# Reordering the opening of a decoder layer: modulation weights, first projection weights, constants and the order of the first products

## The chip, the cores and the metric

The kernel runs on one core of a Trainium2 chip. The metric is device time in microseconds of one execution; before the change the median of three runs is 1246.67 us (1246.11 to 1247.33). All times below are in microseconds unless marked otherwise.

## The reference, cut to what matters

The layer takes x (512 tokens by 1024 channels) and a conditioning vector c. What the change touches is its first step: a layer norm, scaled and shifted by a function of c, then one large projection.

```python
c_act = jax.nn.silu(c)
mod = c_act @ ada_w[l] + ada_b[l]
sh1, sc1, g1, sh2, sc2, g2 = jnp.split(mod, 6, axis=-1)
h = _layer_norm(x) * (1 + sc1[:, None]) + sh1[:, None]
proj = h @ w_in[l] + b_in[l]
```

Behind it stand gated recurrence, sparse attention, a merge, and a mixture of experts; none of their code is changed.

## The kernel before

[...] Tiles come from rings: 36 buffers of 128x1024 floats ("Q"), 24 of 128x512 ("S"), and the 8 banks of PSUM.

**Loads.** The SyncE queue issues, in this order: the four 128-token tiles of x (`xt`), the modulation weights of part 0 (`ada_fetch(0)`, four tiles `adaw` of 512 KB), the first half of the first projection block (`first[0].fetch1()`, 512 KB, four of the eight k-tiles of 128 channels), modulation part 1, the first halves of the second and third block, modulation part 2, the three second halves, modulation part 3, and the block `kw_block`. ScalarE's queue loads c, biases and the table `cst` (identity, triangle, counter: 256.5 KB). GpSimd's queue loads bias rows, then the constants `cmpc` of the later compression step; at the end of the opening stage it also loads `rel_bias` and the bucket table (lines 550 and 554).

**From x to its transpose.** For each x tile VectorE takes statistics (line 229, two halves, then line 231), ScalarE makes the reciprocal deviation (lines 233, 234), VectorE a small product (line 404), ScalarE applies it to the tile (line 405, `x_norm`, line 402). Then `c_silu` runs three small ScalarE steps and three small VectorE steps. Then `x_transposed` (line 407 on) transposes each tile on TensorE; VectorE and ScalarE copy two halves of each bank into `xT` (lines 413, 414). Last come the columns of biases (`colT`, `ncolT`, lines 427, 430).

**Modulation.** `modulation(c)` multiplies silu(c) with the 16 weight pieces of part c. The four pairs of shift or scale (s) and channel half (j) write to four places of 32 columns of the TensorE array, so that products of different places can run side by side. The loop has k outermost, so four neighbouring calls go to four places. VectorE copies the result to `mrow` (line 459); `modulate(c)` brings it into columns by two small products (line 181, `pg<-sel,mrow`) and an addition (line 466, `modc`); ScalarE makes the high part `hh` of two k-tiles of h (line 469), VectorE the full value `hk` (line 471) and the low part `hl` (line 472).

**First products.** Weights are split into high and low parts too (`split1`: ScalarE line 280 gives `wh`, VectorE line 282 gives `wl`). For the first half of `first[0]` the subtraction of line 282 runs on GpSimd. Six PSUM banks `fps` (two for each of three blocks) collect 144 products: for each part c of two k-tiles, for each bank f, the three products wh·hh, wh·hl, wl·hh of both k-tiles, the one with `hl` second. The next modulation is issued ahead of bank 2, its `modulate` ahead of bank 3, so 18 products stand between `modulate(c+1)` and the first product that reads its result.

After that stage follow the products of `kw_block` and, woven in by estimated durations, the compression step and the bias rows (`bias_rows`, line 547 on).

Of the kernel before, what the change touches and what calls it, by code (L numbers as in the profile page):

```python
# [21 lines left out]
F32 = mybir.dt.float32  # L22
F32R = mybir.dt.float32r
# [3 lines left out]
AF = mybir.ActivationFunctionType  # L27
OP = mybir.AluOpType
# [15 lines left out]
C_ID, C_TRI, C_IOTA, C_VAL, C_N = 0, 128, 256, 512, 513  # L44
# [24 lines left out]
MOD_F = 2  # L69
# [71 lines left out]
def hybrid_kernel(ctx, tc, a, out, dbg=None, stop=None):  # L141
    nc = tc.nc
# [7 lines left out]
    cp = ctx.enter_context(tc.tile_pool(name="cp", bufs=1))  # L150
# [5 lines left out]
    def Q(name, dt=F32):  # L156
        return big.tile([128, 1024], dt, name=name, tag="Q", bufs=36)
# [33 lines left out]
    xt = [Q("xt") for i in range(NT)]  # L191
# [4 lines left out]
    A.dma_start(rowa[16:24, :], a["c"][0].rearrange("(r p) -> r p", p=128))  # L196
    A.dma_start(rowa[0:16, :], a["ada_b"][0, 0:2048].rearrange("(r p) -> r p", p=128))
    cst = cp.tile([128, C_N], F32, name="cst")
    A.dma_start(cst, a["cst"])
    A.preload_act_table_set("natural_log_exp_and_others")  # L200

    rows = S("rows")[:, 0:128]
# [5 lines left out]
    P_.dma_start(rows[93:94, :], a["cmp_b1_v"][0][None, :])  # L208

    cmpc = S("cmpc")  # L210
    P_.dma_start(cmpc[:, 0:128], a["cmp_w2_k"][0])
    P_.dma_start(cmpc[:, 128:256], a["cmp_w2_v"][0])
    P_.dma_start(cmpc[0:32, 256:384], a["cmp_pos_k"][0])
    P_.dma_start(cmpc[0:32, 384:512], a["cmp_pos_v"][0])
    ident = cst[:, C_ID:C_ID + 128]
    tri = cst[:, C_TRI:C_TRI + 128]
    iota = cst[:, C_IOTA:C_IOTA + 256]
# [7 lines left out]
    def layer_stats(src, pre, st=None, later=False):  # L225
        if st is None:
            st = small(pre + "st", 12)
            for q in range(2):
                V.bn_stats(st[:, q * 6:(q + 1) * 6], src[:, q * 512:(q + 1) * 512])
        mv = small(pre + "mv", 2, bufs=4 if pre == "l0" else 2)  # L230
        V.bn_aggr(mv, st.rearrange("p (q s) -> p q s", s=6))
        rs = small(pre + "rs", 2, bufs=4 if pre == "l0" else 2)
        A.activation(rs[:, 0:1], mv[:, 1:2], AF.Ln, bias=eps[:, 0:1])
        A.activation(rs[:, 0:1], rs[:, 0:1], AF.Exp, scale=-0.5)
        if not later:
            V.scalar_tensor_tensor(rs[:, 1:2], mv[:, 0:1], -1.0, rs[:, 0:1], op0=OP.mult, op1=OP.mult)
        return mv, rs
# [125 lines left out]
    def ada_fetch(c):  # L363
        t = []
        for s in range(2):
            u = []
            for j in range(2):
                w = Q("adaw").rearrange("p (k n) -> p k n", k=4)
                nc.sync.dma_start(w, ada[:, 4 * j:4 * j + 4, s * 1024 + c * 256:s * 1024 + (c + 1) * 256])
                u.append(w)  # L370
            t.append(u)
        adw.append(t)

    ada_fetch(0)
    first[0].fetch1()
    ada_fetch(1)
    first[1].fetch1()
    first[2].fetch1()
    ada_fetch(2)
    for b in first:  # L380
        b.fetch1()
    ada_fetch(3)
    kw_block = Block(wview, KW)
    kw_block.fetch()

    prow = PS("prow")
    tr(prow[:, 0:24], rowa[:24, :], ident[:24, :24])
# [11 lines left out]
    xT = [Q("xT").rearrange("p (k t) -> p k t", k=2) for _ in range(4)]  # L399
    stats = {}  # L400

    def x_norm(i):
        mv, rs = stats[i]
        V.scalar_tensor_tensor(rs[:, 1:2], mv[:, 0:1], -1.0, rs[:, 0:1], op0=OP.mult, op1=OP.mult)
        A.activation(xt[i], xt[i], AF.Identity, bias=rs[:, 1:2], scale=rs[:, 0:1])

    def x_transposed(i):
        for k4 in range(2):
            pt = PS("pxT")
            for k in range(4):  # L410
                tr(pt[:, k * 128:(k + 1) * 128], xt[i][:, (4 * k4 + k) * 128:(4 * k4 + k + 1) * 128], ident)
            src = pt.rearrange("p (k t) -> p k t", k=4)
            V.tensor_copy(xT[2 * k4][:, :, i * 128:(i + 1) * 128], src[:, 0:2])
            A.activation(xT[2 * k4 + 1][:, :, i * 128:(i + 1) * 128], src[:, 2:4], AF.Copy)
    for i in range(NT):
        stats[i] = layer_stats(xt[i], "l0", later=True)
        if i:
            x_norm(i - 1)
    x_norm(NT - 1)
    c_silu()  # L420
    for i in range(NT):
        x_transposed(i)

    prow2 = PS("prow2")
    tr(prow2[:, :94], rows[:94, :], ident[:94, :94])
    colT = cp.tile([128, 94], F32, name="colT")
    V.tensor_copy(colT, prow2[:, :94])
    b1k, b1v = colT[:, 92:93], colT[:, 93:94]
    ncolT = cp.tile([128, 68], F32, name="ncolT")
    V.tensor_scalar(ncolT, colT[:, :68], -1.0, None, op0=OP.mult)  # L430

    def bcol(off):
        j = off // 128 if off < 6656 else 52 + (off - MGH) // 128
# [3 lines left out]
        j = off // 128 if off < 6656 else 52 + (off - MGH) // 128  # L437
        return ncolT[:, j:j + 1]

    hh = halves("hh")  # L440
    hl = halves("hl")
    modc = cp.tile([128, 2, 8], F32, name="modc")
    fps = [PS("pfirst") for _ in range(6)]
    pg = PS("pg")
    pc = pg[:, 256:272].rearrange("p (k s) -> p s k", s=2)
    mrow = S("mrow")[:, 0:256]

    sel = small("sel", 2, bufs=1)
    V.tensor_add(sel, ident[:, 0:65:64], ident[:, 32:97:64])

    def modulation(c):

        for k in range(4):
            for s in range(2):
                for j in range(2):
                    r = 64 * s + 32 * j
                    mm(pg[r:r + 32, 0:256], cT[:, 4 * j + k:4 * j + k + 1].to_broadcast([128, 32]), adw[c][s][j][:, k, :],
                       k == 0, k == 3, pos=(0, r))
        V.tensor_copy(mrow, pg[:, 0:256])

    def modulate(c):

        for q in range(2):
            mm(pg[:, 256 + 4 * c + 2 * q:258 + 4 * c + 2 * q], mrow[:, q * 128:(q + 1) * 128], sel, True, True)
        cs = slice(2 * c, 2 * c + 2)
        V.tensor_add(modc[:, :, cs], pc[:, :, cs], modb[:, :, cs])
        for k in (2 * c, 2 * c + 1):
            xk = xT[k // 2][:, k % 2, :]
            A.activation(hh(k), xk, AF.Identity, bias=modc[:, 0, k:k + 1], scale=modc[:, 1, k:k + 1])
            hk = S("hk")  # L470
            V.tensor_scalar(hk, xk, modc[:, 1, k:k + 1], modc[:, 0, k:k + 1], op0=OP.mult, op1=OP.add)
            V.tensor_sub(hl(k), hk, hh(k).bitcast(F32))
            if k == 3:
                probe("hk3", hk)

    modulation(0)
    first[0].split1(P_)
    modulate(0)
    for c in range(4):
        if c % 2 == 0:  # L480
            for b in first:
                if len(b.h) <= c // 2:
                    b.split1()
        for f in range(6):
            b = first[f // 2]
            if f % 2 and c == 3 and f < 5:
                kw_block.split1()
            if f == MOD_F and c < 3:
                modulation(c + 1)
            if f == MOD_F + 1 and c < 3:  # L490
                modulate(c + 1)
            for k in (2 * c, 2 * c + 1):
                three_k(fps[f], lambda k: b.H(k, (f % 2) * 128, 128), lambda k: b.L(k, (f % 2) * 128, 128), hh, hl, k)
    probe("modc", modc)


# [50 lines left out]
    def bias_rows():  # L547
        rbT = small("rbT", 8, bufs=1)
        rb = small("rb", 32, bufs=1)
        P_.dma_start(rb[0:8, :], a["rel_bias"])  # L550
        bk = [S("buck") for _ in range(3)]
        for j in range(3):
            wd = 512 if j < 2 else 256
            P_.dma_start(bk[j][0:32, :wd], a["buck"][:, j * 512:j * 512 + wd])
        yield 3000

        def bkc(c, n, rows):
            j, o = divmod(c, 512)
# [12 lines left out]

        P_.dma_start(ext2_d, ext_d[:, None, :].to_broadcast([8, 128, 640]))
# [1265 lines left out]
```

## Time and profile before

| what | value |
|---|---|
| median of three runs | 1246.67 us |
| the profiled execution, own time | 1247.05 us |
| its span, first to last instruction | 1245.3 us |
| mean granted TensorE clock | 0.986 |
| PE busy | 1169.0 us, 94% of the span |
| DVE busy | 685.0 us, 55% |
| ACT busy | 438.4 us, 35% |
| POOL busy | 82.8 us, 7% |

The profile gives one execution. The rows below are read as follows: a line of the timeline is one instruction or a merged run of like ones; the bracket at its end tells how long its engine had stood idle and what released it.

### The profile page before, as it was taken

The numbers are of one execution on the slowest core, as the hardware profiler recorded it, in microseconds if no ns is written. First come the engines' busy times: TensorE is split into PE (matmuls) and PEld (weight loads), VectorE is DVE, ScalarE is ACT, GpSimd is POOL, SyncE is SP. The second block draws the span as 40 slices with busy tenths as digits, with TensorE's granted clock in tenths as the row PEclk, the third lists the DMA queues.
The fourth block names the chain that finished last, engine by engine and source line by source line (L and its number), as shares of the span: only waits on it lengthen the run. The fifth ranks groups of instructions, "written<-read, shape, count | busy, mean of one in ns | idle before, by whom it ended". The sixth has DMA issues, their size and how long they took to land. (4 is left out here: it accounts for less than half of the span.)

```text
span 1245.3 us, 18172 instructions
## 1 busy us (share of the span) xinstructions
PE 1169.0 (94%) x6455; PEld 802.1 (64%) x6455; DVE 685.0 (55%) x1626; ACT 438.4 (35%) x916; POOL 82.8 (7%) x164
## 2 busy tenths in 40 slices
PE   5999999989999999999999979999999899999985
PEld 3788798778888888878877773435435235355322
DVE  5564888787665656322586678435125144444314
ACT  4333656764444353555222541201102001112013
POOL 3011111111011011002000110000000000000000
PEclk9999999999999999999999989999999999999997
DMA  9955324134244234236155199999999999999991
GB/s 325 307 142 156 89 78 127 49 131 133 83 149 122 76 121 136 85 102 194 60 192 169 57 349 348 410 408 410 409 409 408 409 409 409 408 407 401 409 355 71
DMA packets 137629, 296.10 MB, mean 238 GB/s; under 512 B 11195, under 2 KB 74883, under 8 KB 137536
## 3 DMA queue, kind: packets, MB, share of 16 engines
q1 hardware_dynamic: 128224, 268.57, 58.9%
q0 software_dynamic: 8544, 23.97, 6.1%
q10 hardware_dynamic: 768, 2.37, 0.6%
q8 instruction: 52, 0.85, 0.3%
q14 instruction: 41, 0.34, 0.1%
HBM read 292.73 MB, written 4.76 MB: 239 GB/s over the span
## 5 line engine op out<-in xcount | busy, mean ns | idle before, releaser
L183 PE MATMUL p<-ew,xe 128*32 128x512 f32 (+1 forms) x960 | 194.7, 597 | 11.6 <-DMA ew<-in_exp_w_dram 11.6
L282 DVE TENSOR_TENSOR wl<-wst,wh 128x1024 fp32r<-128x1024 f32 (+1 forms) x93 | 109.3, 1201 | 74.2 <-ACT wh L280 73.4
L183 PEld LDWEIGHTS p<-ew,xe 128*32 128x32 f32 (+1 forms) x960 | 53.2, 122 | 146.4 <-issue 83.5
L183 PE MATMUL py<-ew,aT 128*32 128x512 f32 (+1 forms) x464 | 98.6, 598 | 8.7 <-DMA ew<-in_exp_w_dram 5.4
L1545 DVE TENSOR_TENSOR s<-s,p 128x512 f32<-128x512 f32 x13 | 8.9, 688 | 176.4 <-PE p L183 160.7
L280 ACT ACTIVATE wh<-wst 128x1024 fp32r<-128x1024 f32 (+1 forms) x94 | 93.2, 1030 | 29.7 <-DVE wst L271 17.5
L183 PEld LDWEIGHTS py<-ew,aT 128*32 128x32 f32 (+1 forms) x464 | 24.8, 121 | 74.7 <-issue 37.0
L1553 ACT ACTIVATE aT<-pat 128x512 f32<-128x512 f32 x13 | 7.8, 597 | 177.3 <-PE pat L187 177.3
L1594 DVE TENSOR_TENSOR acc<-acc,pcb 128x512 f32<-128x512 f32 x96 | 58.3, 681 | 7.9 <-PE pcb L181 7.9
L1568 ACT ACTIVATE yh<-y 128x512 fp32r<-128x512 f32 x26 | 16.4, 630 | 126.7 <-DVE y L1566 126.7
L181 PE MATMUL pgx<-pm,xhh 128*128 128x256 f32 (+1 forms) x224 | 57.5, 301 | 0.0
L181 PE MATMUL pgx<-pm,xhl 128*128 128x256 f32 (+1 forms) x224 | 55.4, 292 | 0.0
L1566 DVE SCALAR_TENSOR_TENSOR y<-py,cs,g2b 128x512 f32<-128x512 f32 x26 | 19.4, 748 | 57.3 <-PE py L183 57.0
L181 PE MATMUL pmg<-hh,wh 128*128 128x512 f32 x128 | 50.4, 394 | 0.0
L181 PE MATMUL psg<-hh,wh 128*128 128x512 f32 x128 | 50.3, 393 | 0.0
L181 PE MATMUL psg<-hl,wh 128*128 128x512 f32 x128 | 49.9, 390 | 0.0
L181 PE MATMUL psg<-hh,wl 128*128 128x512 f32 x128 | 49.9, 390 | 0.0
L181 PE MATMUL pmg<-hh,wl 128*128 128x512 f32 x128 | 49.8, 389 | 0.0
L181 PE MATMUL pmg<-hl,wh 128*128 128x512 f32 x128 | 49.8, 389 | 0.0
L181 PEld LDWEIGHTS pgx<-pm,xhh 128*128 128x128 f32 x224 | 45.3, 206 | 6.5 <-issue 5.6
L181 PE MATMUL pcb<-yh,pT 128*128 128x512 f32 x104 | 43.7, 420 | 5.3 <-ACT sq L1722 5.3
L521 POOL DMA_DIRECT2D adaw<-in_ada_w_dram x64 | 34.6, 542 | 197.3 <-PE ptp L187 43.4
(552 smaller groups left out, 2777.6 us busy)
## 6 DMA issues: line engine op xcount, KB each, us to landing
ew<-in_exp_w_dram SPq DMA_DIRECT2D x380, 512.0 KB, 10.1
wst<-in_w_in_dram SPq DMA_DIRECT2D x66, 512.0 KB, 4.7
adaw<-in_ada_w_dram POOLq DMA_DIRECT2D x64, 256.0 KB, 3.1
adaw<-in_ada_w_dram SPq DMA_DIRECT2D x16, 512.0 KB, 9.2
wst<-in_w_br_hg_dram SPq DMA_DIRECT2D x8, 512.0 KB, 4.9
wst<-in_w_br_nsa_dram SPq DMA_DIRECT2D x8, 512.0 KB, 3.5
wst<-in_w_out_dram SPq DMA_DIRECT2D x8, 512.0 KB, 5.5
ext_d<-ext_d POOLq DMA_DIRECT2D x1, 2560.0 KB, 17.3
```

What stands on the lines that cost most here:

```text
L181: PE.matmul(o, l, r, start=start, stop=stop)
L183: PE.matmul(o, l, r, start=start, stop=stop, tile_position=pos)
L280: A.activation(wh, self.w[j], AF.Copy)
L282: (sub or V).tensor_sub(wl, self.w[j], wh.bitcast(F32))
L521: P_.dma_start(w, ada[:, k, 2048 + j * 512:2560 + j * 512])
L1545: V.tensor_mul(s1, s1, p3)
L1553: A.activation(aT, at_.rearrange("p (f s) -> p f s", f=4), AF.Copy)
L1566: V.scalar_tensor_tensor(y, py, cs_, g2b[c0 // 512][:, c0 % 512:c0 % 512 + n], op0=OP.mult, op1=OP.mult)
L1568: A.activation(yh, y, AF.Copy)
L1594: V.tensor_add(acc[i][:, s_], acc[i][:, s_], pc_)
```

## The change

- The first half of `first[0]` is loaded in two parts of two k-tiles (256 KB each). The first part goes ahead of modulation part 0, the second behind the first halves of the other two blocks; these three go ahead of modulation part 1. The parts are split one by one (`f0_split`), by ScalarE and VectorE; GpSimd does no subtraction any more.
- ScalarE's queue loads only the identity of `cst` (64 KB). The rest of it and `cmpc` are loaded by SyncE's queue behind `kw_block`. `rel_bias` and the bucket table are loaded by SyncE's queue too.
- The order from x to its transpose: the small product and the shift of tile i-1 stand between the two statistics halves of tile i; `c_silu` stands between tile 2 and tile 3; transposes and copies of tile 0 precede the shift of tile 3; `f0_split(0)` stands ahead of the copies of tile 3.
- `modulation` has k innermost, so that the four products of one place follow one another. In part 0 its copy to `mrow` and the addition into `modc` are made in two pieces.
- The products go by pairs of banks: for each k-tile wh·hh for both banks, then wl·hh, then wh·hl. The next modulation is issued ahead of banks 2 and 3 (in part 0 ahead of banks 4 and 5), its `modulate` behind the first k-tile of that pair.

```diff
-    A.dma_start(cst, a["cst"])
+    A.dma_start(cst[:, :C_TRI], a["cst"][:, :C_TRI])
...
+    def late_constants():
+        nc.sync.dma_start(cst[:, C_TRI:], a["cst"][:, C_TRI:])
+        nc.sync.dma_start(cmpc[:, 0:128], a["cmp_w2_k"][0])
...
+    def f0_fetch(k):
+        nc.sync.dma_start(f0w[:, k:k + 2], wview[:, k:k + 2, KC:KC + 256])
+
+    def f0_split(k):
+        A.activation(f0h[:, k:k + 2], f0w[:, k:k + 2], AF.Copy)
+        V.tensor_sub(f0l[:, k:k + 2], f0w[:, k:k + 2], f0h[:, k:k + 2].bitcast(F32))
+
+    f0_fetch(0)
     ada_fetch(0)
-    first[0].fetch1()
-    ada_fetch(1)
+    first[0].w.append(f0w)
     first[1].fetch1()
     first[2].fetch1()
+    f0_fetch(2)
+    ada_fetch(1)
     ada_fetch(2)
...
     kw_block.fetch()
+    late_constants()
...
+    def x_stats(i):
+        st = small("l0st", 12)
+        for q in range(2):
+            V.bn_stats(st[:, q * 6:(q + 1) * 6], xt[i][:, q * 512:(q + 1) * 512])
+            if q == 0 and i:
+                x_shift(i - 1)
+        stats[i] = layer_stats(xt[i], "l0", st=st, later=True)
...
-    for i in range(NT):
-        stats[i] = layer_stats(xt[i], "l0", later=True)
-        if i:
-            x_norm(i - 1)
-    x_norm(NT - 1)
+    x_stats(0)
+    x_stats(1)
+
+    V.tensor_add(sel, ident[:, 0:65:64], ident[:, 32:97:64])
+    x_stats(2)
     c_silu()
-    for i in range(NT):
-        x_transposed(i)
-
+    x_stats(3)
+    x_transposed(0)
+    x_shift(3)
+    x_transposed(1)
     prow2 = PS("prow2")
     tr(prow2[:, :94], rows[:94, :], ident[:94, :94])
+    pg = PS("pg")
+    x_transposed(2)
...
+    f0_split(0)
...
+    x_transposed(3)
     V.tensor_copy(colT, prow2[:, :94])
+    V.tensor_scalar(ncolT, colT[:, :68], -1.0, None, op0=OP.mult)
...
     def modulation(c):
 
-        for k in range(4):
-            for s in range(2):
-                for j in range(2):
-                    r = 64 * s + 32 * j
+        for s in range(2):
+            for j in range(2):
+                r = 64 * s + 32 * j
+                for k in range(4):
                     mm(pg[r:r + 32, 0:256], cT[:, 4 * j + k:4 * j + k + 1].to_broadcast([128, 32]), adw[c][s][j][:, k, :],
                        k == 0, k == 3, pos=(0, r))
-        V.tensor_copy(mrow, pg[:, 0:256])
+        for q in range(1 if c else 2):
+            w = slice(0, 256) if c else slice(q * 128, (q + 1) * 128)
+            V.tensor_copy(mrow[:, w], pg[:, w])
...
+    def first_products(fs, k, js=range(3)):
+
+        for j in js:
+            for f in fs:
+                b, w = first[f // 2], (f % 2) * 128
+                l, r = ((b.H, hh), (b.L, hh), (b.H, hl))[j]
+                mm(fps[f], l(k, w, 128), r(k), start=k == 0 and j == 0, stop=k == KT - 1 and j == 2)
+
     modulation(0)
-    first[0].split1(P_)
     modulate(0)
     for c in range(4):
-        if c % 2 == 0:
+        if c == 0:
+            first[1].split1()
+            first[2].split1()
+        if c == 2:
             for b in first:
-                if len(b.h) <= c // 2:
-                    b.split1()
...
+        for f in range(0, 6, 2):
+            if f == (2 if c else 4) and c < 3:
+                modulation(c + 1)
+            if f == 2 and c == 0:
+                f0_split(2)
...
             for k in (2 * c, 2 * c + 1):
-                three_k(fps[f], lambda k: b.H(k, (f % 2) * 128, 128), lambda k: b.L(k, (f % 2) * 128, 128), hh, hl, k)
+                first_products((f, f + 1), k)
+                if f == (2 if c else 4) and k == 2 * c and c < 3:
+                    modulate(c + 1)
...
-        P_.dma_start(rb[0:8, :], a["rel_bias"])
+        nc.sync.dma_start(rb[0:8, :], a["rel_bias"])
...
-            P_.dma_start(bk[j][0:32, :wd], a["buck"][:, j * 512:j * 512 + wd])
+            nc.sync.dma_start(bk[j][0:32, :wd], a["buck"][:, j * 512:j * 512 + wd])
```

## Rows read from the trace of the kernel before

**Rows 1.** The page: its first line, and from its second part the busy tenths of TensorE in 40 equal slices of the span.

```profile
span 1245.3 us, 18172 instructions
...
PE   5999999989999999999999979999999899999985
```

**Rows 2.** Busy time by stretches of the span. Columns: stretch in us, its length, busy us and instructions in brackets of PE, PEld, DVE, ACT and POOL, granted TensorE clock as a share of full speed, DMA share, GB/s.

```profile
0.00:16.40 16.40, 6.51 (x34) 4.94 (x34) 7.73 (x26) 9.03 (x19) 5.45 (x14) 1.00 0.92 312
16.40:27.10 10.70, 7.28 (x48) 4.66 (x48) 7.43 (x15) 5.80 (x11) 4.48 (x5) 0.84 1.11 344
27.10:61.80 34.70, 34.70 (x229) 26.49 (x229) 19.47 (x37) 10.28 (x13) 0.00 (x0) 1.00 1.05 313
```

**Rows 3.** Who waited for whom between 0 and 55 us: waiting engine, tile and line, what it waited for; us in total, times, longest.

```profile
DVE cT L394 <- ACT ce L243: 2.6, 1, 2.6
...
PE pfirst L181 <- DVE hl L472: 1.8, 1, 1.8
```

**Rows 4.** The timeline from the end of the first modulation to the second one. Columns: start us, duration us, engine, line, operation, output and input, shape, count, idle time before it with its releaser.

```profile
18.42 0.42 DVE L459 COPY mrow<-pg 128x256 f32<-128x256 f32 x1
...
19.39 2.35 POOL L282 TENSOR_TENSOR wl<-wst,wh 128x1024 fp32r<-128x1024 f32 x1 [11.11 <-ACT wh L280]
19.55 0.16 DVE L466 TENSOR_TENSOR modc<-pg,modb 128x4 f32<-128x4 f32 x1 [0.70 <-PE pg L181]
19.75 1.52 ACT L469 ACTIVATE hh<-xT,modc 128x512 fp32r<-128x512 f32 x2 [0.45 <-DVE modc L466]
19.75 2.27 DVE L471 TENSOR_SCALAR hk<-xT,modc 128x512 f32<-128x512 f32 x1
...
20.61 0.50 PE L181 MATMUL pfirst<-hh,wh 128*128 128x512 f32 x1 [1.10 <-ACT hh L469]
...
22.73 0.54 DVE L471 TENSOR_SCALAR hk<-xT,modc 128x512 f32<-128x512 f32 x1
...
22.87 0.80 PE L181 MATMUL pfirst<-hl,wh 128*128 128x512 f32 x1 [1.75 <-DVE hl L472]
...
27.14 1.93 PE L183 MATMUL pg<-adaw,cT 128*32 128x256 f32 x32
...
29.00 0.50 PE L181 MATMUL pfirst<-hh,wh 128*128 128x512 f32 x1
```

**Rows 5.** Busy time by stretches, columns as in Rows 2, around the time when the granted clock changed.

```profile
22.50:23.00 0.50, 0.13 (x1) 0.14 (x1) 0.50 (x2) 0.00 (x0) 0.50 (x2) 0.81 1.10 346
23.00:26.00 3.00, 3.00 (x7) 2.21 (x8) 0.96 (x2) 0.76 (x1) 0.86 (x2) 0.50 1.10 348
26.00:26.50 0.50, 0.50 (x3) 0.44 (x2) 0.17 (x1) 0.30 (x1) 0.00 (x0) 0.78 1.14 365
```

**Rows 6.** The timeline of the way from x to the transposed x (statistics, shift, sigmoid, copies), columns as in Rows 4.

```profile
6.03 0.29 ACT L233 ACTIVATE l0rs<-l0mv,eps 128x1 f32<-128x1 f32 x1 [2.58 <-DVE l0mv L231]
6.35 0.20 ACT L234 ACTIVATE l0rs<-l0rs 128x1 f32<-128x1 f32 x1
...
8.20 1.29 DVE L229 BATCH_NORM_STATS2 l0st<-xt 128x6 f32<-128x512 f32 x2 [0.74 <-DMA xt<-in_x_dram]
...
12.04 2.36 ACT L405 ACTIVATE xt<-xt,l0rs 128x1024 f32<-128x1024 f32 x2
...
14.31 0.15 ACT L241 ACTIVATE ce<-prow 128x8 f32<-128x8 f32 x1
...
14.98 0.16 DVE L394 TENSOR_TENSOR cT<-ce,prow 128x8 f32<-128x8 f32 x1 [2.65 <-ACT ce L243]
...
15.65 2.70 ACT L414 ACTIVATE xT<-pxT 128x256 f32<-128x256 f32 x8 [0.71 <-DVE xT L413]
...
17.86 0.25 DVE L427 COPY colT<-prow 128x94 f32<-128x94 f32 x1
```

**Rows 7.** The products of the first modulation: its row of the timeline; stretches of 0.05 us with the records of line 183 in flight in brackets, PE first and weight loads (PEld) second; then, from the timeline of a later stage, ten records of 128 columns that share one place in the array.

```profile
16.42 1.93 PE L183 MATMUL pg<-adaw,cT 128*32 128x256 f32 x32
...
16.60:16.65 0.05, 0.05 (x4) 0.00 (x0) 1.00 1.17 369
16.65:16.70 0.05, 0.05 (x8) 0.04 (x4) 1.00 1.14 348
16.80:16.85 0.05, 0.05 (x8) 0.00 (x0) 1.00 1.13 348
...
16.90:16.95 0.05, 0.05 (x8) 0.05 (x4) 1.00 1.16 369
...
72.00 1.25 PE L181 MATMUL pext<-buck,rbT 32*8 32x128 f32 x10
```

**Rows 8.** Transfers: the last tile of the first modulation's weights (issue, then time to landing, the answer for that tile between 6.5 and 8.5 us), two splits that waited for their weights, the SyncE queue's issues for the compression weights, and the first transpose that needs the bias table.

```profile
L369 SPq DMA_DIRECT2D adaw<-in_ada_w_dram x1: 2293/2293/2293, 5.6 to 5.6; - x1
...
DMA to landing us min/median/max: 10.6/10.6/10.6
...
25.24 1.06 ACT L280 ACTIVATE wh<-wst 128x1024 fp32r<-128x1024 f32 x1 [3.98 <-DMA wst<-in_w_in_dram]
...
26.78 1.06 ACT L280 ACTIVATE wh<-wst 128x1024 fp32r<-128x1024 f32 x1 [0.48 <-DMA wst<-in_w_in_dram]
...
45.97 6.96 SPq L261 DMA_DIRECT2D wst<-in_cmp_w_k_dram  x4
...
70.22 0.18 PE L187 MATMUL prb<-cst,rb 8*32 8x8 f32 x1
```

More of the change, by code (lines that the diff above doesn't have):

```diff
@@ L210, in hybrid_kernel @@
     cmpc = S("cmpc")
[L211 to L214, printed above, removed]
+    def late_constants():
+        nc.sync.dma_start(cst[:, C_TRI:], a["cst"][:, C_TRI:])
+        nc.sync.dma_start(cmpc[:, 0:128], a["cmp_w2_k"][0])
+        nc.sync.dma_start(cmpc[:, 128:256], a["cmp_w2_v"][0])
+        nc.sync.dma_start(cmpc[0:32, 256:384], a["cmp_pos_k"][0])
+        nc.sync.dma_start(cmpc[0:32, 384:512], a["cmp_pos_v"][0])
     ident = cst[:, C_ID:C_ID + 128]
@@ L372, in ada_fetch @@
         adw.append(t)
+    f0w = Q("wst").rearrange("p (k n) -> p k n", k=4)
+    f0h = f0l = None
+    def f0_fetch(k):
[4 more added lines that the diff above has]
+    f0_fetch(0)
     ada_fetch(0)
-    first[0].fetch1()
-    ada_fetch(1)
+    first[0].w.append(f0w)
     first[1].fetch1()
     first[2].fetch1()
+    f0_fetch(2)
+    ada_fetch(1)
     ada_fetch(2)
@@ L400, in hybrid_kernel, with x_shift @@
     stats = {}
-    def x_norm(i):
+    def x_stats(i):
[5 more added lines that the diff above has]
+        stats[i] = layer_stats(xt[i], "l0", st=st, later=True)
+    def x_shift(i):
         mv, rs = stats[i]
@@ L414, in x_transposed @@
             A.activation(xT[2 * k4 + 1][:, :, i * 128:(i + 1) * 128], src[:, 2:4], AF.Copy)
-    for i in range(NT):
-        stats[i] = layer_stats(xt[i], "l0", later=True)
-        if i:
-            x_norm(i - 1)
-    x_norm(NT - 1)
+    sel = small("sel", 2, bufs=1)
+    colT = cp.tile([128, 94], F32, name="colT")
+    ncolT = cp.tile([128, 68], F32, name="ncolT")
+    x_stats(0)
+    x_stats(1)
+    V.tensor_add(sel, ident[:, 0:65:64], ident[:, 32:97:64])
+    x_stats(2)
     c_silu()
-    for i in range(NT):
-        x_transposed(i)
+    x_stats(3)
+    x_transposed(0)
+    x_shift(3)
+    x_transposed(1)
     prow2 = PS("prow2")
     tr(prow2[:, :94], rows[:94, :], ident[:94, :94])
-    colT = cp.tile([128, 94], F32, name="colT")
+    pg = PS("pg")
+    x_transposed(2)
+    hh = halves("hh")
+    f0h = Q("wh", F32R).rearrange("p (k n) -> p k n", k=4)
+    f0l = Q("wl", F32R).rearrange("p (k n) -> p k n", k=4)
+    f0_split(0)
+    first[0].h.append(f0h)
+    first[0].l.append(f0l)
+    x_transposed(3)
     V.tensor_copy(colT, prow2[:, :94])
+    V.tensor_scalar(ncolT, colT[:, :68], -1.0, None, op0=OP.mult)
     b1k, b1v = colT[:, 92:93], colT[:, 93:94]
-    ncolT = cp.tile([128, 68], F32, name="ncolT")
-    V.tensor_scalar(ncolT, colT[:, :68], -1.0, None, op0=OP.mult)
     def bcol(off):
@@ L438, in nbcol @@
         return ncolT[:, j:j + 1]
-    hh = halves("hh")
     hl = halves("hl")
@@ L443, in hybrid_kernel @@
     fps = [PS("pfirst") for _ in range(6)]
-    pg = PS("pg")
     pc = pg[:, 256:272].rearrange("p (k s) -> p s k", s=2)
     mrow = S("mrow")[:, 0:256]
-    sel = small("sel", 2, bufs=1)
-    V.tensor_add(sel, ident[:, 0:65:64], ident[:, 32:97:64])
     def modulation(c):
-        for k in range(4):
-            for s in range(2):
-                for j in range(2):
-                    r = 64 * s + 32 * j
+        for s in range(2):
+            for j in range(2):
+                r = 64 * s + 32 * j
+                for k in range(4):
                     mm(pg[r:r + 32, 0:256], cT[:, 4 * j + k:4 * j + k + 1].to_broadcast([128, 32]), adw[c][s][j][:, k, :],
                        k == 0, k == 3, pos=(0, r))
-        V.tensor_copy(mrow, pg[:, 0:256])
+        for q in range(1 if c else 2):
+            w = slice(0, 256) if c else slice(q * 128, (q + 1) * 128)
+            V.tensor_copy(mrow[:, w], pg[:, w])
     def modulate(c):
@@ L464, in modulate @@
             mm(pg[:, 256 + 4 * c + 2 * q:258 + 4 * c + 2 * q], mrow[:, q * 128:(q + 1) * 128], sel, True, True)
-        cs = slice(2 * c, 2 * c + 2)
-        V.tensor_add(modc[:, :, cs], pc[:, :, cs], modb[:, :, cs])
+        for cs in ([slice(2 * c, 2 * c + 2)] if c else [slice(0, 1), slice(1, 2)]):
+            V.tensor_add(modc[:, :, cs], pc[:, :, cs], modb[:, :, cs])
         for k in (2 * c, 2 * c + 1):
@@ L474, in modulate @@
                 probe("hk3", hk)
+    def first_products(fs, k, js=range(3)):
[4 more added lines that the diff above has]
+                mm(fps[f], l(k, w, 128), r(k), start=k == 0 and j == 0, stop=k == KT - 1 and j == 2)
     modulation(0)
-    first[0].split1(P_)
     modulate(0)
     for c in range(4):
-        if c % 2 == 0:
+        if c == 0:
+            first[1].split1()
+            first[2].split1()
+        if c == 2:
             for b in first:
-                if len(b.h) <= c // 2:
-                    b.split1()
-        for f in range(6):
-            b = first[f // 2]
-            if f % 2 and c == 3 and f < 5:
+                b.split1()
+        for f in range(0, 6, 2):
[3 more added lines that the diff above has]
+                f0_split(2)
+            if f and c == 3:
                 kw_block.split1()
[L488 to L491, printed above, removed]
             for k in (2 * c, 2 * c + 1):
-                three_k(fps[f], lambda k: b.H(k, (f % 2) * 128, 128), lambda k: b.L(k, (f % 2) * 128, 128), hh, hl, k)
+                first_products((f, f + 1), k)
+                if f == (2 if c else 4) and k == 2 * c and c < 3:
+                    modulate(c + 1)
     probe("modc", modc)
```

## The prediction

> **What bounds the kernel now.** I read the page first: TensorE is busy in nine tenths of nearly every slice, and the first slice, with 5, is the emptiest but the last [rows 1]. The change touches only work that ends near 62 us. The stretches show where that part has air: up to 27.1 us TensorE works 6.51 of 16.40 and 7.28 of 10.70 us, in the second at a mean granted clock of 0.84; from 27.1 to 61.8 us it is busy all the time at full clock [rows 2]. What TensorE starts earlier by 27.1 us moves the rest forward. I take it that this reaches the end one for one: each later stage waits for the one before, and I found no clock time that a later stage is tied to.
>
> The list of waits names what TensorE missed behind its first product: the low part `hl`, 1.8 us [rows 3]. The timeline says why `hl` was late: GpSimd's subtraction ran from 19.39 for 2.35 us, and the `hk` step of VectorE that began inside it took 2.27 us, the next one, outside it, 0.54 [rows 4]. So the first product began at 20.61, the second at 22.87. [...] Transfers run at full load here (DMA share 1.11 [rows 2]), but no product waited for one.
>
> My reference point is therefore: product 12 is done at 27.1 in the run of 1247.05 us, whose span is 1245.3 us. The median, 1246.67, is 0.38 lower; the result is set against the median.
>
> **The change, part by part.** *When can the first product start?* Three chains have to be walked in the new program order.
>
> Transfers. By part 0 of the modulation, 256 KB more (the first half-block part) and about 350 KB less (constants) have been asked for. Two 512 KB loads land 1.54 us apart [rows 8], so the last modulation tile, which landed at 5.6 + 10.6 = 16.2 us [rows 8], lands about 0.3 us earlier, near 15.9; its three companions some 1.5 us apart before it. The x tiles lose 190 KB of competition, at most 0.5 us: I let the third land at 7.85 instead of 8.20 [rows 6].
>
> VectorE and ScalarE. The second shift now needs only the first half of tile 2's statistics: 7.85 + 0.64 (half of 1.29) + 0.2 = 8.7; ScalarE shifts until 9.95 (1.18 each, 2.36 for two), takes the deviation until 10.45 (0.52, from 6.03 to 6.55) and the sigmoid until 11.1 (0.67, 14.31 to 14.98) [rows 6]. VectorE waits for that sigmoid now as it did before (2.6 us [rows 3]), but with tile 3's statistics queued behind it: cT and its companions end at 11.35, the statistics (1.29 and 0.3 of small steps) at 13.0. That is the stall the new order brings. ScalarE then has, in a row: deviation of tile 3 until 13.9, two copies of tile 0 (0.34 each, 2.70 for eight [rows 6]) to 14.6, shift 3 to 15.8, four copies to 17.1, the high half of the first weights (between 0.53, half of 1.06 [rows 8], and 0.76, half of 1.52 [rows 4]; I take 0.62) to 17.75. VectorE: low half (0.69 as for `hl`: no row for this shape, bounded by 0.54 [rows 4] below and half of GpSimd's 2.35 above; I take 0.69, nearer the VectorE row) to 18.45, two copies to 19.15, `colT` and `ncolT` (0.25 [rows 6] and a little less) to 19.6, half of `mrow` (0.28 of 0.42 [rows 4]) to 19.9. These column copies, hidden behind the modulation before, are now on the path. From the end of `mrow` to `modc` was 18.84 to 19.71, 0.87; then 0.76 for `hh` and 0.1 to the product: 21.6. Hence the first product starts 1.0 us later than before, by 0.8 to 1.4 with the bounds above.
>
> TensorE. The transposes of tile 3 follow shift 3; ScalarE ends it at 15.8, so I let them end at 16.6 (an estimate; up to 18 it would change nothing). All modulation tiles have landed by then, so the landing order gains nothing. If the modulation still takes 1.93 us [rows 7] it ends at 18.6, a microsecond before VectorE can copy it.
>
> *From the first product to the twelfth.* With the low part third and nothing on GpSimd, `hl` is ready 1.6 us behind `modc` (0.54 for `hk` beside the 0.76 of `hh`, then 0.69); the product that needs it is the fifth, 0.95 + 4 x 0.23 = 1.9 us behind `modc` at full clock. [...] No stall of 1.8 us then. Twelve products take 2.75 us at full clock: 24.4, against 27.1, a gain of 2.7. If the clock drops for the 3.4 us that it was low before [rows 5], eight products run at 0.43 instead of 0.23, 1.6 us more: a gain of 1.1. TensorE idles 3 us ahead of the first product now, against 4.5 (18.35 [rows 7] to 22.87 [rows 4], with two small products and one full one inside) before the fall in the old trace. Either is possible; 1.1 and 2.7 are the ends, less the 0.4 by which the start may be later.
>
> *Modulations 1 to 3.* Their 32 records each are on TensorE's dense path (27.14 to 29.0 [rows 4]). In the old order neighbours go to four places. With k innermost the eight records of one place come in a row. Rows 7 show four records in flight, then eight as the next four join at 16.65, with four weight loads at 16.65 and four at 16.9: one place takes a new record each 0.22 us ((1.93 - 0.38) / 7; the ten records in one place give (1.25 - 0.27) / 9 = 0.11 for half the columns), and the four places advance together. In program order a call's second record and its weight load stand ahead of the next call's first; yet the first records of four calls start at once, and the next call's load for place 2 goes out 0.22 us ahead of the second load for place 1. So a record that waits for its place doesn't stop records of other places behind it, at least three instructions deep. How deep this goes no row shows. Bounds: 0 if it reaches over 16 instructions, and 3 x 8 x 0.22 = 5.3 us for each modulation if it didn't exist. I take 0 to 0.3, nearest to the overlap that rows 7 show.
>
> [...]
>
> *The rest.* `modulate(1)` now has six products (1.36 us) behind it instead of 18. From its small products to `hh` takes 1.5 us and to the first low part 2.3 (`mrow` to `modc` and the steps above); the products come at 0.36 + 1.36 = 1.7 and, low part third, 2.6 us. It fits by 0.2 and 0.3 us; without that cover it would cost those tenths once. The last tile of modulation 1 was asked for one 512 KB load ahead of the weights that landed at 25.24 [rows 8], so it landed near 23.7; now 1 MB more goes ahead of it (3.1 us) and the constants don't (1.0): 25.8, and TensorE asks for it at 27 or later. SyncE's queue takes nine more issues; the bias table goes out near 46 us, ahead of the compression weights [rows 8], lands some 9 us later and is needed at 70.22 [rows 8]: hidden by over 10 us. Constants, too. GpSimd's empty queue speeds nothing else.
>
> Sum of the likeliest case: 2.7 to 1.1 gained at the twelfth product, less up to 0.4 for a late start and 0 to 0.9 for the modulations: a gain between -0.2 and 2.7, centre 1.4. 1246.67 - 1.4 = 1245.3.
>
> **Rivals.**
>
> *Places block each other.* If a place with waiting records holds up all behind it, three times the wait of six records comes on top: 3 x 6 x 0.22 = 4.0 us for each modulation, 5.3 at worst. The first one then ends at 22.6, the first product starts at 24.6 and the twelfth ends at 27.4; three more modulations cost 12. Together +12.3, 1259.0 us, chance 0.20. [...] A partial depth gives 1248 to 1257, chance 0.10. It decides from the point at which TensorE looks ahead less than one place's 16 instructions. For it: nothing in the trace looks that far. Against it: rows 7.
>
> *The modulation does run as its tiles land.* If VectorE's and ScalarE's chain is shorter than I walked it (done by 17.6, when the last tile's four products could end), the first product starts at 19.6 and the twelfth ends between 22.4 and 24: a gain of 3.1 to 4.7, 1242.0 to 1243.6. Against it: the sigmoid in VectorE's queue and the row of ScalarE steps behind it.
>
> *It doesn't do what it says.* The start is later by 1 us and the clock stays low longer: no difference; this is inside the likeliest case.
>
> **How the numbers follow.** Chance of the likeliest case 0.55, of blocked places (whole or partial) 0.36, of the quick chain 0.09. A measurement of this kernel tells about 0.2%, 2.5 us, from no change. In the likeliest case the gain exceeds that one time in seven: faster 0.08 + 0.09 = 0.17, same 0.47, slower 0.36. The likeliest case alone spans 1244.0 to 1246.9. Since cases of both signs count, the range reaches from 1243.6 over it to the blocked places, 1259.5; most of the quick chain and the full 5.3 us are left out.
>
> **What would show it.** Right: one modulation from 27 us on still lasts about 1.9 us; `hk` takes 0.54 at once; the first product starts at 21.6 with VectorE's `colT` just ahead of `mrow`; no wait for `hl`. Wrong: a modulation of 5 to 7 us (places block); a first product before 20 us (quick chain); a wait of TensorE for `hh` of part 1, or for the bias table near 70 us.

## The result and the profile after

The changed kernel takes 1260.94 us in the median (1257.22 to 1261.41), the kernel before, run beside it, 1246.95: a ratio of 1.0104 [1.0091, 1.0118], slower by 1%. The profiled execution took 1257.22 us (span 1255.4), 10.2 more than that of before (1247.05). It was the quickest of the four, and the account below is of its 10.2 us. A later measurement of the same kernel (the last run of experiment 1) gave 1258.4 us, ratio 1.0089 [1.0071, 1.0106].

The timeline of the changed kernel, from the statistics of tile 3 to the first products. It answers to [rows 4, 6]; columns as there.

```profile
8.32 0.16 DVE L446 TENSOR_TENSOR sel<-cst 128x2 f32<-128x2 f32 x1 [0.89 <-DMA cst<-in_cst_dram]
...
11.42 0.16 DVE L411 TENSOR_TENSOR cT<-ce,prow 128x8 f32<-128x8 f32 x1 [1.43 <-ACT ce L246]
11.64 0.68 DVE L422 BATCH_NORM_STATS2 l0st<-xt 128x6 f32<-128x512 f32 x1
...
13.72 1.09 PE L187 MATMUL pxT<-cst,xt 128*128 128x128 f32 x8 [1.34 <-ACT xt L430]
...
15.81 1.97 PE L187 MATMUL pxT<-cst,xt 128*128 128x128 f32 x8 [1.00 <-ACT xt L430]
...
17.70 5.13 PE L183 MATMUL pg<-adaw,cT 128*32 128x256 f32 x32
...
22.88 0.49 DVE L491 COPY mrow<-pg 128x128 f32<-128x128 f32 x2 [3.72 <-PE pg L183]
...
24.26 0.55 DVE L503 TENSOR_SCALAR hk<-xT,modc 128x512 f32<-128x512 f32 x1
...
25.13 0.79 PE L181 MATMUL pfirst<-hh,wh 128*128 128x512 f32 x2 [1.10 <-ACT hh L501]
...
29.58 0.63 PE L181 MATMUL pfirst<-hh,wh 128*128 128x512 f32 x2
```

And TensorE's timeline of the changed kernel from 32 to 78 us: the three later modulations and the first product of the next stage (`pk`, at 64.7 us in the trace of before).

```profile
32.43 4.59 PE L183 MATMUL pg<-adaw,cT 128*32 128x256 f32 x32
43.12 4.59 PE L183 MATMUL pg<-adaw,cT 128*32 128x256 f32 x32
56.53 4.59 PE L183 MATMUL pg<-adaw,cT 128*32 128x256 f32 x32
75.29 0.39 PE L181 MATMUL pk<-hh,wh 128*128 128x512 f32 x1
```

A modulation of 32 records took 1.93 us before [rows 4, 7]; now it takes 4.59, at full clock (1.00 in the steps below). Three times 2.66 is 8.0 us. The first one, partly at half clock (0.50 from 16 to 18 us, 0.58 from 18 to 19), takes 5.13 and starts 1.3 us later, so the first product comes 4.5 us later than in [rows 4]; the wait for `hl` is gone, so behind the twelfth product 2.4 of these are left (29.58, where the thirteenth begins, against 27.14 [rows 4]). 8.0 + 2.4 = 10.4, and `pk` is 10.6 us late. Later stages pass this on almost whole: the last stage's `pcl` starts 10.8 us later in the two traces (1238.56 against 1227.80).

Why 4.59? The changed kernel's second modulation from 43.1 us in steps of 0.1 us, line 183 alone: in brackets the records in flight, PE first, then weight loads; then granted clock, DMA share, GB/s.

```profile
43.10:43.20 0.10, 0.09 (x1) 0.09 (x2) 1.00 1.07 338
...
43.90:44.00 0.10, 0.10 (x2) 0.00 (x0) 1.00 1.06 333
...
44.30:44.40 0.10, 0.10 (x4) 0.06 (x2) 1.00 0.97 303
...
46.30:46.40 0.10, 0.10 (x4) 0.06 (x2) 1.00 0.02 5
...
47.10:47.20 0.10, 0.10 (x2) 0.09 (x1) 1.00 0.00 0
...
47.50:47.60 0.10, 0.10 (x1) 0.00 (x0) 1.00 0.00 0
```

It begins and ends with one or two records in flight, where [rows 7] has four and then eight almost from the start. The places no longer run together; each starts some time after the one before it.

### The profile page after: what moved, and what is told of

The parts are those of the page before. It is cut to its first block, busy times and chain, and to the rows that moved or that the text cites. A ratio compares the mean times of both kernels' runs of the same rounds, so it can differ in the third digit from the quotient of the medians.

```text
span 1255.4 us, 18176 instructions
## 1 busy us (share of the span) xinstructions
PE 1181.6 (94%) x6455; PEld 808.0 (64%) x6455; DVE 684.5 (55%) x1630; ACT 437.5 (35%) x917; POOL 76.2 (6%) x155
## 5 line engine op out<-in xcount | busy, mean ns | idle before, releaser
L283 ACT ACTIVATE wh<-wst 128x1024 fp32r<-128x1024 f32 (+1 forms) x93 | 92.0, 1029 | 25.9 <-DVE wst L274 17.5
## 6 DMA issues: line engine op xcount, KB each, us to landing
ext_d<-ext_d POOLq DMA_DIRECT2D x1, 2560.0 KB, 17.2
```

The source lines that it names most:

```text
L283: A.activation(wh, self.w[j], AF.Copy)
```

## Experiments

**1. Which part costs?** The theory after the first trace: a place takes up a few records and then holds up what stands behind. Rival: the 10 us come from the changed opening. The changed kernel with k outermost again; with runs of two products per place; the kernel before with k innermost alone; and the changed kernel once more. Where a diff shows only added lines, here and in experiment 2, it writes the loop order as nested loops; the kernel spells the same order in one line.

```diff
 # modulation of the changed kernel, k outermost again
-        for s in range(2):
-            for j in range(2):
-                r = 64 * s + 32 * j
-                for k in range(4):
+        for k in range(4):
+            for s in range(2):
+                for j in range(2):
+                    r = 64 * s + 32 * j
```

```diff
 # the changed kernel, runs of two products in a place
+        for ks in ((0, 1), (2, 3)):
+            for s in range(2):
+                for j in range(2):
+                    for k in ks:
```

```diff
 # the kernel before, with the loop of the changed one
-        for k in range(4):
-            for s in range(2):
-                for j in range(2):
+        for s in range(2):
+            for j in range(2):
+                for k in range(4):
```

k outermost: 

> The changed kernel with the modulation loop as it was (k outermost, neighbouring products in four places), all else as changed. Theory (places block each other): each of modulations 1 to 3 goes back from 4.59 to about 1.93 us, the first from 5.13 to about 2, and the first product starts 2.5 to 3.5 us earlier than at 25.1; together 10 to 12 us less than the changed kernel, 1246 to 1250. Rival (the new order of x, constants and SyncE's queue costs the time): the modulations shorten, but the time stays above 1253.

Runs of two: 

> The changed kernel with runs of two products per place instead of four (each place is visited twice). Theory (a place holds one running record and three waiting ones; the queue passes on to the next place when a run's rest fits): two products are four records, which fit, so a modulation lasts 1.9 to 2.2 us and the time is that of k outermost within 1 us. Rival (any run of one place blocks the rest until it is over): each change of place overlaps by one record only, 8 runs of 4 records, a modulation lasts about 5.5 us, and the time is as slow as the changed kernel or slower.

Before with k innermost: 

> The kernel before with k innermost in the modulation alone. Theory: three modulations 2.66 us longer each, 8.0 us, and the first one 2.7 us later with the first product; part of that hides under the wait for the low part that GpSimd holds up until 22 us, so 8 to 11 us slower than before, 1255 to 1258. Rival (blocking matters only with the new order): within 2 us of before.

The changed kernel again: 

> The changed kernel once more, unaltered, because its profiled execution took 1257.2 us and three others 1260.8 to 1261.4. If the time has two levels, this run shows both again, and a profile of the slower one may show where the 4 us lie; if the first was a stray, all runs lie near 1261.

| run | median us | ratio to before | modulations 1 to 3 | first product | `pk` |
|---|---|---|---|---|---|
| before, first profile | 1246.86 beside these | 1 | 1.93 | 20.61 | 64.69 |
| changed, k outermost | 1246.86 | 1.0002 [0.9985, 1.0018] | 1.93 | 22.40 | 64.58 |
| changed, runs of two | 1248.25 | 1.0006 [0.9992, 1.002] | 1.97 | 22.11 | 62.65 |
| before, k innermost | 1256.45 | 1.0072 [1.0053, 1.0092] | 4.59 | 23.19 | 74.2 |
| changed, again | 1258.4 | 1.0089 [1.0071, 1.0106] | 4.59 | 24.72 | 74.9 |

One later modulation of the version with k outermost:

```profile
37.72 1.93 PE L183 MATMUL pg<-adaw,cT 128*32 128x256 f32 x32
```

From the timeline of the version with runs of two: the column copies, the copy into `mrow` and a later modulation.

```profile
18.98 0.20 DVE L465 TENSOR_SCALAR ncolT<-colT 128x68 f32<-128x68 f32 x1
...
19.85 0.49 DVE L490 COPY mrow<-pg 128x128 f32<-128x128 f32 x2 [0.67 <-PE pg L183]
...
35.84 1.97 PE L183 MATMUL pg<-adaw,cT 128*32 128x256 f32 x32
```

TensorE's timeline of the kernel before with k innermost:

```profile
16.37 4.59 PE L183 MATMUL pg<-adaw,cT 128*32 128x256 f32 x32
28.61 4.59 PE L183 MATMUL pg<-adaw,cT 128*32 128x256 f32 x32
42.01 4.59 PE L183 MATMUL pg<-adaw,cT 128*32 128x256 f32 x32
```

The loop order alone carries the loss: put into the kernel before it costs about what the whole change costs (1.0072 and 1.0089, with intervals that overlap), and taken out of the change it leaves no difference that can be measured. Runs of two cost next to nothing, which a run of four didn't let one guess. Of the rest of the change the k-outermost version gains nothing at `pk`, the version with runs of two 2.0 us; the second kept full clock from 22 to 30 us (1.00), the first did not (0.57 from 22 to 26, 1.00 from 26 to 30). The medians do not show these 2.0 us: that of runs of two lies 1.4 above that of k outermost, where I had expected less than 1, but the twelve times of each spread over 8 to 10 us. The changed kernel's second measurement spreads from 1256.56 to 1261.07 without a gap between two levels, and its profile (1256.75) again caught a quick execution. Stretches of k outermost and of runs of two, in this order (columns as in [rows 2]):

```profile
22.00:26.00 4.00, 3.60 (x9) 2.83 (x10) 3.60 (x6) 3.47 (x5) 0.00 (x0) 0.57 1.10 348
```

```profile
22.00:26.00 4.00, 3.89 (x17) 3.24 (x18) 3.81 (x5) 3.18 (x5) 0.00 (x0) 1.00 1.10 348
```

**2. How deep?** A run of n products in a place is 2n records, one each 0.22 us ((1.93 - 0.38) / 7 from [rows 7]). If a place holds four (one runs, three wait), each record of a run above four keeps TensorE 0.22 us from going on to the next place. Two sizes between test this: runs of three, and two places that alternate for all their products before the other two begin.

```diff
 # runs of three, then the fourth products
+        for ks in ((0, 1, 2), (3,)):
+            for s in range(2):
+                for j in range(2):
+                    for k in ks:
```

```diff
 # two places in turn
+        for s in range(2):
+            for k in range(4):
+                for j in range(2):
```

Runs of three: 

> The changed kernel with runs of three products in one place, then the fourth products of all places. Theory (a place holds four records, so runs of two cost nothing and a run of four costs 2.7 us): two of the six records of each run are beyond the depth; a modulation takes 3.1 to 3.4 us. Rival (a whole run blocks what stands behind it): over 4 us. Runs of two had taken 1.97.

Two places in turn: 

> The changed kernel with two places in turn: the eight products of places 1 and 2 alternate, then those of 3 and 4. Theory (the depth counts per place): the third place starts when both first places have at most four records left, half of eight; 0.88 + 0.22 x 7 + 0.38 = 2.8 us per modulation (2.7 to 3.0). Rival (the depth is a count over all places): either 1.95 (never full) or 4 us and more.

One line of the second modulation of each, runs of three first:

```profile
30.44 3.30 PE L183 MATMUL pg<-adaw,cT 128*32 128x256 f32 x32
```

```profile
28.46 2.82 PE L183 MATMUL pg<-adaw,cT 128*32 128x256 f32 x32
```

With a depth of four the sums are: run of two 1.93; three 1.93 + 3 x 2 x 0.22 = 3.25; four 1.93 + 3 x 4 x 0.22 = 4.57; two places in turn 1.93 + 4 x 0.22 = 2.81. Measured 1.97, 3.30, 4.59, 2.82. One depth of four records for each place fits all four; a whole run that blocks fits none. Nor does one count over all places: reckoned in the same way, with 0.22 us for a record, five in all would give 4.6 for runs of four, but 3.2 for runs of two (estimates). Since every product here is two records, the runs do not tell four records from two products. And products of different places did not start in the order of the program: with runs of two a modulation took 1.97 us, for which records had to start past others that waited for another place. `pk` came at 69.3 and 65.9 us, the times were 1251.93 and 1248.83.

**3. Does the order by tile gain anything as tiles land?** The changed kernel with k innermost in modulation 0 alone.

```diff
+        for s, j, k in ([(s, j, k) for s in range(2) for j in range(2) for k in range(4)] if c == 0 else
+                        [(s, j, k) for k in range(4) for s in range(2) for j in range(2)]):
```

> The changed kernel with k innermost in modulation 0 alone (by tile as it lands) and outermost in modulations 1 to 3. Theory (all four tiles have landed before the modulation can start, so the order by tile gains nothing and the queue of four records costs): modulation 0 takes 4.6 to 5.1 us, the first product starts at 24.7 to 25.1, modulations 1 to 3 take 1.93, 1247 to 1250 us. Rival (the order by tile starts earlier): first product before 22.4, under 1246 us.

TensorE's timeline of this run:

```profile
17.53 4.59 PE L183 MATMUL pg<-adaw,cT 128*32 128x256 f32 x32
...
24.42 1.22 PE L181 MATMUL pfirst<-hh,wh 128*128 128x512 f32 x2 [1.10 <-ACT hh L501]
```

1249.62 us, modulation 0 at 4.59 and the first product at 24.42, 0.3 earlier than I expected. There was nothing to gain: no transfer is waited for. And where one is (experiment 5), it is the last tile; its eight records in one place take about 1.9 us after it has landed (7 x 0.22 + 0.38), whatever the order of the others.

**4. What sets the first product?** Both versions with short modulations start their products at 22.1 to 22.4, later than either profile of before (20.61, 21.92). The prediction put this down to VectorE's queue; the copy into `mrow` of the version with runs of two waits 0.67 us for `pg`, though, which speaks for TensorE's own chain (shift 3, transposes of tile 3, modulation). Test: in that version `f0_split(0)` moved behind `modulation(0)`.

```diff
-    f0_split(0)          # ahead of x_transposed(3)
...
     modulation(0)
+    f0_split(0)
```

> Runs of two products per place, and one more step moved: the first split of weights (its high and low part) stands behind modulation 0 instead of ahead of the copies of tile 3. Theory (TensorE's own chain binds: shift 3, transposes of tile 3, modulation, all ahead of the copy into mrow): the first product stays at 22.0 to 22.4, the copy waits for pg. Rival (VectorE's queue binds, as the prediction had it): without the 0.69 of the low part the first product comes at 21.5 or earlier.

The timeline of this run:

```profile
17.33 1.97 PE L183 MATMUL pg<-adaw,cT 128*32 128x256 f32 x32
...
19.38 0.49 DVE L489 COPY mrow<-pg 128x128 f32<-128x128 f32 x2 [1.13 <-PE pg L183]
...
21.63 0.73 PE L181 MATMUL pfirst<-hh,wh 128*128 128x512 f32 x2 [1.10 <-ACT hh L499]
```

The first product came at 21.63, between the two expectations. VectorE now waits 1.13 us for TensorE, so its queue does not bind; but the modulation itself began 0.41 earlier (17.33 against 17.74), as the last transposes ran faster, and this is nearly all of the 0.48 by which the first product came earlier. For the faster transposes I have no shown cause (see the last section); the two runs were also on different chips. 1247.84 us.

**5. The opening in another order.** With k outermost: the sigmoid's VectorE steps behind tile 3's statistics, shifts 2 and 3 back to back ahead of the copies, the first split behind modulation 0.

```diff
     def c_silu():
-        sigmoid(ce, prow[:, 16:24], 0.0)
...
-            if q == 0 and i:
+            if q == 0 and i in (1, 2):
                 x_shift(i - 1)
...
     x_stats(0)
     x_stats(1)
+    sigmoid(ce, prow[:, 16:24], 0.0)
+    x_stats(2)
+    x_stats(3)
+    x_shift(2)
+    x_shift(3)
     V.tensor_add(sel, ident[:, 0:65:64], ident[:, 32:97:64])
-    x_stats(2)
     c_silu()
-    x_stats(3)
     x_transposed(0)
-    x_shift(3)
     x_transposed(1)
...
-    f0_split(0)
...
     modulation(0)
+    f0_split(0)
```

> The changed kernel with k outermost again, and with the way from x to the first product reordered: the sigmoid's ScalarE steps right behind tile 1's statistics, its VectorE steps and sel behind tile 3's statistics (so that the statistics of tile 3 no longer stand behind them), shifts 2 and 3 back to back ahead of the copies, the first split of weights behind modulation 0. Theory (what ate the gain is the first product that comes 1.5 to 2 us later than before): first product near 20.3 us (19.8 to 20.8), pk near 60.5 to 62.5, 1242.5 to 1245 us. Rival (these steps don't bound the chain): first product at 22 or later, 1246 to 1248 us.

TensorE's timeline of this run, from modulation 0 to the first product:

```profile
14.92 0.63 PE L183 MATMUL pg<-adaw,cT 128*32 128x256 f32 x6
...
15.86 1.91 PE L183 MATMUL pg<-adaw,cT 128*32 128x256 f32 x26 [0.31 <-DMA adaw<-in_ada_w_dram]
...
20.06 0.74 PE L181 MATMUL pfirst<-hh,wh 128*128 128x512 f32 x2 [1.10 <-ACT hh L500]
```

The chain moved as expected: first product at 20.06, `pk` at 60.65 (4.0 us ahead of before), 1243.66 us in the profiled run. The median is 1245.67, above the expected 1242.5 to 1245, ratio 0.999 [0.9976, 1.0004]: not shown to beat before. Its twelve times fall into two groups, six of 1242.31 to 1244.92 at a mean granted clock of 0.988 to 0.989 and six of 1246.42 to 1248.65 at 0.985 to 0.986. To see where the two differ I profiled it twice more, and before once more.

> The reordered opening once more, unchanged, for a second profile. Theory (its times fall into two groups 4 us apart by the mean granted clock, 0.988 to 0.989 and 0.985 to 0.986; the order of the opening is the same in both): first product at 20.0 to 20.2 and pk at 60.6 if TensorE stays at full clock up to 30 us, pk 1 to 2 us later if the clock falls there; the rest of the difference shows as further stretches of 10 us with a granted clock under 1. Rival (the opening itself varies, by its transfers): a first product at 21 or later.

> The same kernel a third time; the same is expected as of the second profile.

> The kernel before once more, for a second profile of it. Theory (the fall of the clock at 23 to 26 us belongs to this order, which leaves TensorE idle ahead of its first products): the clock is again at half there, pk at 64.7. Rival (the fall is chance): full clock, pk 1 to 2 us earlier.

The reordered opening took 1243.02 and 1241.41 us. The wait for the last tile ended at 16.27 and 16.62, the first product began at 20.47 and 20.82, `pk` at 61.03 and 61.45, all at full clock (1.00) from 14 to 30 us. So the first product varied by 0.76, more than I expected, and in all three profiles it stood 4.20 us behind the end of the wait for the last modulation tile: the transfers bind now. No profile caught an execution of the upper group, so where that group loses its 4 us stays open. Within the three profiles the times do not follow `pk` (61.45 goes with the shortest); cut into stretches of 10 us, the three traces have 8, 7 and 5 of them with a granted clock under 1, all from 150 us on, in the order of their times; three executions are too few to make this a cause.

Before took 1248.91 us. Its third x tile landed later than in [rows 6], and the whole opening came later (timeline, then stretches of the same run):

```profile
8.88 1.29 DVE L229 BATCH_NORM_STATS2 l0st<-xt 128x6 f32<-128x512 f32 x2 [1.45 <-DMA xt<-in_x_dram]
...
12.16 5.38 PE L187 MATMUL pxT<-cst,xt 128*128 128x128 f32 x24 [0.80 <-ACT xt L405]
...
19.73 0.42 DVE L459 COPY mrow<-pg 128x256 f32<-128x256 f32 x1 [0.88 <-PE pg L183]
...
21.92 0.51 PE L181 MATMUL pfirst<-hh,wh 128*128 128x512 f32 x1 [1.10 <-ACT hh L469]
...
23.31 0.50 PE L181 MATMUL pfirst<-hl,wh 128*128 128x512 f32 x1 [0.88 <-DVE hl L472]
```

```profile
22.00:24.00 2.00, 1.12 (x4) 0.59 (x4) 1.79 (x4) 0.57 (x1) 2.00 (x5) 1.00 1.10 348
24.00:25.00 1.00, 0.70 (x3) 0.40 (x2) 0.51 (x1) 0.00 (x0) 0.30 (x1) 0.85 1.11 349
25.00:26.00 1.00, 1.00 (x4) 0.75 (x3) 0.00 (x0) 0.17 (x1) 0.00 (x0) 0.50 1.11 349
26.00:28.00 2.00, 2.00 (x6) 1.22 (x4) 1.07 (x1) 0.94 (x2) 0.00 (x0) 0.50 1.12 311
```

0.68 us at the x tile became 1.3 at the first product. The transposes account for the growth: the 24 of tiles 1 to 3 ran from 12.16 to 17.54, one each 0.22 us, where the first profile of before took 1.79 us for twelve of its own, one each 0.15, as this line of it shows:

```profile
13.32 1.79 PE L187 MATMUL pxT<-cst,xt 128*128 128x128 f32 x12 [0.24 <-ACT xt L405]
```

So modulation 0 began at 17.63 instead of 16.42, and the copy into `mrow` waited 0.88 us for it. The wait for `hl` was 1.2 us in two pieces instead of 1.8, and the clock fell again (0.50 from 25 to 28 us), about 2 us later than in [rows 5]. `pk` came at 65.72. The reference point of the prediction was thus one draw of an opening that moves by about a microsecond, and the fall of the clock there was seen a second time.

## Why the prediction was wrong

The step that failed is "Modulations 1 to 3": "I take 0 to 0.3, nearest to the overlap that rows 7 show." They cost 2.66 us each. [Rows 7] showed records of other places starting past waiting ones, at least three instructions deep; I took the depth as open and then put the likeliest value at the end where it is deep enough. But in the order of before each place is handed two records at a time before the next place has its turn, so that trace asks for no greater depth and could not show one. Experiment 2 measured it: four records for each place (or two products), not a count over all places. The rival "places block each other" said that it decides "from the point at which TensorE looks ahead less than one place's 16 instructions"; that condition was right: four records and their weight loads are eight instructions. Its price for the whole place (4.0) was too high, and the case that came, a partial depth at 1248 to 1257, had a chance of 0.10. The odds of 0.55 to 0.36 for the deep case had no row behind them.

That the time still came out at or above this case's upper end has other reasons. The prediction's own walk with 4.59 in place of 1.93 ends its twelfth product at 25.9 (16.6 + 4.59 + 2.0 + 2.75), 1.2 ahead of before, and loses 8.0 later: +6.8, 1253.5. In the profile the thirteenth product begins at 29.58, another 3.6 later: modulation 0 began 1.1 late, its half clock cost 0.5, the way from `mrow` to the product 0.3, and the twelve products took 4.45 instead of 2.75, mostly at half clock (0.83 from 25 to 26 us, 0.50 from 26 to 29).

The other steps:

- Modulation 0 "1.93, 16.6 to 18.6": it began at 17.2 to 17.7 in the versions that keep the changed opening, and with k outermost it took 2.89, with the clock at half (0.50 from 16 to 18 us). That the transposes "up to 18" would change nothing was wrong: with runs of two the modulation ends at 19.8, after `ncolT` (19.18), and the copy into `mrow` waits for it. VectorE's queue, which the prediction held to be the bound, ended 0.4 earlier than walked.
- The first product at 21.6: 22.1 and 22.4 with short modulations. From `mrow` to the product it is 2.26 us (19.85 to 22.11), not 2.0. The sum was nearly right, by another chain.
- No stall for `hl`, `hk` at once: 0.55 us, and no product waited for `hl` in any version of the change. Right.
- "Either is possible" for the clock, gains of 1.1 and 2.7: with runs of two and full clock (1.00 from 22 to 26 us) `pk` is 2.0 ahead, with k outermost and a clock of 0.57 there 0.1 ahead. Right in kind; the lower end was 0.1 and not 1.1. The 0.23 us for a product at full clock, in these gains and in the sum for `hl`, was an estimate that no row shows. What the runs showed: in the trace of before six products in 1.36 us at 1.00 (31.17 to 32.53); for the first twelve, up to the start of the thirteenth, 2.85 us with runs of two (22.11 to 24.96) against the 2.75 reckoned, and 4.44 with k outermost (22.40 to 26.84) against 4.35.
- Fewer bytes ahead of the first tiles: `cst` landed at 8.3 instead of 8.6, though it was asked for 64 KB in place of 256.5, and `sel`, moved ahead of tile 2's statistics, waited 0.89 us for it. I had not walked that; the statistics of tile 3 still ended at 13.0 (13.2 with their small step), as predicted.
- Weights, constants, the bias table: no product waited for any of them. Right.
- One for one to the end: 10.6 us at `pk`, 10.8 in the last stage. Right. The median, though, is 14.0 above that of before in the first measurement and 11.5 in the second. Both profiles of the changed kernel caught quick executions (1257.22 and 1256.75), so where the others lose up to 4 us more, and what the 2.5 between the medians are, is not settled.

## What to carry to other kernels

Where f32 products go to several column places, the length of the run in one place is worth a measurement. Here, with four places of 32 columns, a modulation took 1.93 us when neighbouring products went to four places, 1.97 with runs of two, 3.30 with runs of three and 4.59 with runs of four; for each record above four the next place began 0.22 us later, by the sums of experiment 2. A trace bounds a queue's depth only up to what its program has asked of it: if no row goes deeper, no row speaks for the deep case over the shallow one. And this opening, bound by transfers and by several engines in turn, moved by a microsecond between profiles (first product at 20.61 and 21.92 in before), so a gain of 2 us there needs several profiles of both kernels.

## What the runs showed of the hardware that was not expected

- A depth of four records, or two products, per column place fits the four times of experiment 2 (1.97, 3.30, 4.59 and 2.82 us). A modulation of 16 products is 32 records of 256 columns, two for a product, and one place took a record each 0.22 us.
- The eight transposes of tile 3 took 1.97 us from 15.8 us, with the granted clock at 0.50 in the changed kernel; with runs of two they took the same time with a clock recorded as 1.00. Those of tile 2, both times at a recorded 1.00, took 1.09 in the changed kernel and 1.97 with runs of two. The recorded clock and the pace do not agree there; I have no explanation. In both profiles of before, too, the first transposes are slow at a recorded 1.00 (tile 0: 1.97 us from 9.19 in the first), and how soon they turn quick differs, at 12 to 13 us in the first profile and not before 17.5 in the second. So in these profiles a recorded 1.00 in the first 18 us did not mean full pace. The stretch of the changed kernel:

```profile
16.00:18.00 2.00, 2.00 (x9) 1.56 (x9) 0.60 (x1) 1.37 (x5) 0.00 (x0) 0.50 1.11 350
```

- In the changed kernel the clock fell twice, at 16 to 18 us and at 26 to 29, the second time after a stretch (22 to 25 us) in which TensorE worked 1.45 of 3 us:

```profile
22.00:25.00 3.00, 1.45 (x8) 0.74 (x6) 1.23 (x5) 0.74 (x2) 0.00 (x0) 1.00 1.10 348
...
26.00:29.00 3.00, 3.00 (x8) 2.32 (x8) 2.90 (x4) 2.20 (x3) 0.00 (x0) 0.50 1.10 348
```
